# Modulation rows of the second block: products and sums on ACT, GpSimd and VectorE, with TensorE summing over the partitions

## The chip, the cores and the metric

One core of a Trainium2 chip runs the whole program. The metric is the time of one execution on the device in microseconds. Engines are named as in the profile: PE is TensorE (PEld its weight load), DVE is VectorE, ACT is ScalarE, POOL is GpSimd, SP is SyncE, whose queue issues most loads.

## The reference

The program computes two transformer blocks in float32. The first has two layers of a mixer and a SwiGLU FFN (512 tokens, width 1024, FFN width 2816). The second works on the result and on 256 context tokens, with a modulation of each of its two layers:

```python
silu_c, silu_cc = jax.nn.silu(c), jax.nn.silu(c_ctx)
for i in range(DEPTH):                      # 2 layers
    mod_l = silu_c @ ada_w[i] + ada_b[i]    # ada_w[i]: 1024 x 6144
    mod_c = silu_cc @ ada_w[i] + ada_b[i]
    sh1, sc1, gt1, sh2, sc2, gt2 = jnp.split(mod_l[:, None, :], 6, axis=-1)
    ...
```

So for each layer two vectors are multiplied with one matrix of 1024 rows and 6144 columns (24 MB). The inputs c and c_ctx do not depend on the first block, and the result is first needed in the second block.

## The kernel before, in words

The matrix is worked off inside the first block. `ada` (L1040) is a generator: each `next` sends one unit. For a layer there are 24 blocks of 256 columns. A unit loads one block of 1 MB (`adaw`, two buffers, one DMA on SP's queue), and sends eight matmuls on PE (L1053), one per group of 128 rows, with 32 columns of `cs` as the stationary operand (column 0 is silu(c), column 1 silu(c_ctx), the others zero). They go to four column groups of PE, so the result has four partial sums in four groups of 32 partitions. DVE copies it to `adap` (L1058). The next `next` sums the four groups and turns the row into a column by two matmuls with `sel` (L1061), and DVE adds the bias into `modT` (L1062). After the 24 blocks it scales and stores some rows, loads the router of the layer's mixture of experts (MoE), and folds the modulation into the router's bias.

The units are sent from `ada_step` (L1034), which `gemm_t` (L270) calls once per f-step. An f-step is one output tile of 128 columns by 512 tokens: 24 product matmuls, since each float32 product is made of three (L266 with xH and wH, L267 with xL and wH, L268 with xH and wL), for eight groups of 128 rows. Three of four f-steps send a unit, and one generator runs through both layers. The calls are in `ffn` (L525 and after), in the loop over blocks of the gate and the up weights. There, ACT makes the high part of a weight tile (L244) and DVE the low part (L245). For a gate tile DVE multiplies with the norm's factor (L530), ACT applies silu (L531), POOL multiplies with the factor once more (L532); for an up tile DVE multiplies into it (L535). The product tiles in PSUM are four buffers named `mmps`.

The order in which each engine gets its instructions is set by the scheduler of the framework, which moves units ahead of where the code sends them: in both kernels the first units of a layer stand before its FFN. For layer 0 that is the gated linear attention of the first mixer, GLA (lines L725 to L834), the output projection after it, and the residual (L359, L360, L370, L371, with a sum of squares by ACT L2800 and POOL L2807, the sum over partitions by PE L2820, the root by ACT L2811 and the reciprocal by DVE L2812, which gives `rstd`, the factor of the FFN's norm).

The lines that the steps of the prediction touch are those named here, and in GLA the ACT table loads at L729 and L730, DVE L731 to L744, POOL L746 and L749, and DVE L827.

## Time and profile before

| | before |
|---|---|
| median of 3 runs | 4202.54 us (4191.84 to 4209.45) |
| profiled execution | 4201.93 us |
| span of its trace | 4200.0 us |
| busy, PE | 3774.0 us (90%) |
| busy, DVE | 1838.8 us (44%) |
| busy, ACT | 1322.6 us (31%) |
| busy, POOL | 683.8 us (16%) |
| loads of the modulation matrix | 48 of 1024 KB, 5.0 us from issue to landing |

The span is the time between the first and the last instruction in the trace; 1.93 us lie around it. Busy shares are averages over stages with quite different limits, so each stage is read by itself. The line of an instruction is that of the kernel's file; a helper such as `mm3` has one line for all its callers, so the names of the tiles tell them apart. PE's matmuls are pipelined: what one costs is read from the distance between starts, not from its length.

### The profile page before, as it was taken

The numbers are of one execution on the slowest core, as the hardware profiler recorded it, in microseconds if no ns is written. First come the engines' busy times: TensorE is split into PE (matmuls) and PEld (weight loads), VectorE is DVE, ScalarE is ACT, GpSimd is POOL, SyncE is SP. The second block draws the span as 40 slices with busy tenths as digits, with TensorE's granted clock in tenths as the row PEclk, the third lists the DMA queues.
The fourth block names the chain that finished last, engine by engine and source line by source line (L and its number), as shares of the span: only waits on it lengthen the run. The fifth ranks groups of instructions, "written<-read, shape, count | busy, mean of one in ns | idle before, by whom it ended". The sixth has DMA issues, their size and how long they took to land. (4 is left out here: it accounts for less than half of the span.)

```text
span 4200.0 us, 56465 instructions
## 1 busy us (share of the span) xinstructions
PE 3774.0 (90%) x22550; PEld 2588.1 (62%) x22550; DVE 1838.8 (44%) x3646; ACT 1322.6 (31%) x2612; POOL 683.8 (16%) x889
## 2 busy tenths in 40 slices
PE   7979999999999979998789997996788899688986
PEld 6747778756777869887333334774667777433332
DVE  3445345565534545334422225445657655511112
ACT  3334224344323433233111113424456555200001
POOL 1002000200201010001100002002555342200001
PEclk9969999999999989999899998997768769799998
DMA  3213553212452322122799996342211212499997
GB/s 110 81 38 117 182 192 105 81 32 76 144 179 82 101 70 68 52 102 79 294 406 391 398 404 236 93 152 66 54 40 43 60 48 79 185 394 415 415 413 306
DMA packets 324825, 711.86 MB, mean 169 GB/s; under 512 B 79616, under 2 KB 251904, under 8 KB 299728
## 3 DMA queue, kind: packets, MB, share of 16 engines
q1 hardware_dynamic: 308704, 658.43, 43.1%
q0 software_dynamic: 15856, 49.79, 3.4%
q8 instruction: 179, 2.93, 0.3%
q14 instruction: 86, 0.70, 0.1%
HBM read 666.64 MB, written 47.55 MB: 170 GB/s over the span
## 5 line engine op out<-in xcount | busy, mean ns | idle before, releaser
L266 PE MATMUL mmps<-xH,wH 128*128 128x512 f32 (+1 forms) x1384 | 552.0, 401 | 11.2 <-ACT xH L359 9.4
L268 PE MATMUL mmps<-xH,wL 128*128 128x512 f32 (+1 forms) x1384 | 543.9, 394 | 2.4 <-DVE wL L245 2.4
L267 PE MATMUL mmps<-xL,wH 128*128 128x512 f32 (+1 forms) x1384 | 544.8, 394 | 0.0
L1488 PE MATMUL bgps<-wg,bxT 128*64 128x512 f32 (+2 forms) x1040 | 471.5, 597 | 0.9 <-issue 0.9
L1489 PE MATMUL bgps<-wu,bxT 128*64 128x512 f32 (+1 forms) x896 | 398.2, 597 | 21.1 <-DMA wu<-in_moe_w_up_dram 20.8
L244 ACT ACTIVATE wH<-wraw 128x512 fp32r<-128x512 f32 (+3 forms) x473 | 265.0, 620 | 481.4 <-PE mmps L267 270.6
L245 DVE TENSOR_TENSOR wL<-wraw,wH 128x512 fp32r<-128x512 f32 (+3 forms) x473 | 328.6, 739 | 193.6 <-ACT wH L244 193.0
L266 PEld LDWEIGHTS mmps<-xH,wH 128*128 128x128 f32 (+1 forms) x1384 | 259.9, 188 | 92.4 <-ACT wH L244 12.4
L268 PEld LDWEIGHTS mmps<-xH,wL 128*128 128x128 f32 (+1 forms) x1384 | 259.9, 188 | 66.1 <-DVE wL L245 3.9
L1505 PE MATMUL byps<-wd,bhT 128*64 128x512 f32 (+2 forms) x1040 | 297.0, 658 | 1.1 <-ACT bhT L1496 1.1
L267 PEld LDWEIGHTS mmps<-xL,wH 128*128 128x128 f32 (+1 forms) x1384 | 260.2, 188 | 59.9 <-issue 1.4
L1488 PEld LDWEIGHTS bgps<-wg,bxT 128*64 128x64 f32 (+2 forms) x1040 | 139.0, 137 | 206.7 <-issue 200.3
L1490 ACT ACTIVATE bh<-bgps 64x512 f32<-64x512 f32 (+2 forms) x65 | 38.3, 590 | 641.2 <-PE bgps L1489 543.0
L1489 PEld LDWEIGHTS bgps<-wu,bxT 128*64 128x64 f32 (+1 forms) x896 | 111.9, 128 | 132.7 <-issue 91.6
L1491 DVE TENSOR_TENSOR bh<-bgps,bh 64x512 f32<-64x512 f32 (+1 forms) x56 | 38.6, 690 | 335.7 <-ACT bh L1490 335.7
L1505 PEld LDWEIGHTS byps<-wd,bhT 128*64 128x64 f32 (+2 forms) x1040 | 87.9, 147 | 157.8 <-issue 152.1
L2420 POOL TENSOR_TENSOR isub<-xT,rwX 96x31 f32<-96x31 f32 (+15 forms) x248 | 140.6, 567 | 262.0 <-DMA xT<-rwd 243.2
L1454 POOL DMA_INDIRECT xg<-hnat,ix x65 | 62.8, 967 | 640.1 <-PE bxps L1476 602.9
L2424 POOL TENSOR_TENSOR rwX<-rwX,isub 96x31 f32<-96x31 f32 (+15 forms) x248 | 155.5, 627 | 19.4
L2807 POOL TENSOR_TENSOR sqs<-sqs,sq 128x512 f32<-128x512 f32 (+1 forms) x60 | 82.3, 1372 | 392.8 <-ACT sq L2800 386.4
L266 PE MATMUL mmps<-mH,pH 128*128 128x512 f32 (+2 forms) x336 | 124.1, 372 | 12.0 <-ACT pH L244 9.1
L532 POOL TENSOR_TENSOR ffng<-ffng,rstd 128x512 f32<-128x512 f32 x44 | 57.8, 1316 | 452.2 <-ACT ffng L531 439.9
(746 smaller groups left out, 7529.6 us busy)
## 6 DMA issues: line engine op xcount, KB each, us to landing
wg<-in_moe_w_gate_dram SPq DMA_DIRECT2D x64, 2048.0 KB, 23.1
wu<-in_moe_w_up_dram SPq DMA_DIRECT2D x61, 2048.0 KB, 20.1
wd<-in_moe_w_down_dram SPq DMA_DIRECT2D x61, 2048.0 KB, 19.2
adaw<-in_ada_w_dram SPq DMA_DIRECT2D x48, 1024.0 KB, 5.0
wraw<-in_ffn_w_gate_dram SPq DMA_DIRECT2D x22, 1024.0 KB, 5.4
wraw<-in_ffn_w_up_dram SPq DMA_DIRECT2D x22, 1024.0 KB, 5.5
wraw<-in_ffn_w_down_dram SPq DMA_DIRECT2D x20, 1024.0 KB, 5.0
wraw<-in_ga_w_in_dram SPq DMA_DIRECT2D x16, 1024.0 KB, 5.5
```

The source lines that it names most:

```text
L244: self.nc.scalar.activation(H, src, AF.Copy)
L245: self.nc.vector.tensor_tensor(L, src, H.bitcast(F32), OP.subtract)
L266: nc.tensor.matmul(out, lh, rh, start=first, stop=False)
L267: nc.tensor.matmul(out, lh, rl, start=False, stop=False)
L268: nc.tensor.matmul(out, ll, rh, start=False, stop=last)
L1454: self.gathered = self.nc.gpsimd.indirect_dma_start(out=x[:m, :], out_offset=None, in_=hnat, in_offset=bass.IndirectOffsetOnAxis(ap=it, ax ...
L1488: nc.tensor.matmul(og, xT[:, k, :m], wg[:, k, :], start=k == 0, stop=k == KD - 1, skip_group_check=True)
L1489: nc.tensor.matmul(ou, xT[:, k, :m], wu[:, k, :], start=k == 0, stop=k == KD - 1, skip_group_check=True)
L1505: nc.tensor.matmul(o[j], hT[:, k, :m], wd[:, k, j * 512 : (j + 1) * 512], start=k == 0, stop=k == 3, skip_group_check=True)
L2420: G.tensor_tensor(o, Lt[:96, :j, j : j + 1].to_broadcast((96, j, n)), X[:96, j : j + 1, j:].to_broadcast((96, j, n)), OP.mult,)
L2424: G.tensor_tensor(X[:96, :j, j:], X[:96, :j, j:], o, OP.add)
L2807: K.nc.gpsimd.tensor_tensor(self.acc, self.acc, t, OP.add)
```

## The change

The row sums move from PE to the other engines. A block has 512 columns now, 12 per layer, and is loaded in eight pieces of 128 rows (256 KB each, four buffers). For each piece ACT multiplies the tile by silu(c) of its rows (L1080), POOL adds that to `adac0` (L1081), and DVE multiplies by silu(c_ctx) and adds to `adac1` in one instruction (L1082); the first piece of a block is written by ACT (L1076) and DVE (L1077) directly. `adac0` and `adac1` have one buffer each. When a block is complete, PE sums both over the partitions by two matmuls with ones (L1052), ACT copies the result (L1054), and after a `yield` PE transposes it in four pieces (L1058) and DVE adds the bias (L1059). Each layer has its own generator, which must end in its own FFN, and an f-step sends one or two units of two pieces each. Lines of the changed kernel are one higher from the FFN on, and 23 higher behind `ada` (L2800, L2807, L2811, L2812 are now L2823, L2830, L2834, L2835).

```diff
@@ -539,12 +539,13 @@
                 (ev_gate, ev_up)[j // 2](j % 2, ps)
             ca = c.enter_context(ExitStack())
             self.adap = self.pool(f"ada{l}", ctx=ca)
+            self.ada_todo = self.ada(l)
             for b in range(256, FF, 256):
                 self.gemm_t(wg, b, b + 256, x, evac=lambda i, ps: ev_gate(b // P + i, ps), step=self.ada_step)
                 self.gemm_t(wu, b, b + 256, x, evac=lambda i, ps: ev_up(b // P + i, ps), step=self.ada_step)
+            assert next(self.ada_todo, self) is self
+            ca.close()
             if nxt is None:
-                assert next(self.ada_todo, self) is self
-                ca.close()
                 self.start_ctx()
             yp = self.pool(f"yffn{l}", ctx=c)
             yT = yp.tile([P, KD, T], F32, name="yT2")
@@ -1024,7 +1025,6 @@
         nc.scalar.activation(self.cs[:, :, 0], self.pvc("c_2", 0, 8), AF.Silu)
         nc.scalar.activation(self.cs[:, :, 1], self.pvc("c_ctx_2", 0, 8), AF.Silu)
         self.ada_n = 0
-        self.ada_todo = (u for l in range(2) for u in self.ada(l))
         late = self.cs.rearrange("p k i -> p (k i)")
         self.Lg, self.rtok = late[:, : TA // P * 36].rearrange("p (t e) -> p t e", e=36), late[:, TA // P * 36 : TA // P * 37]
         rcl = mp.tile([P, 2, 2, 36], F32, name="rcl")
@@ -1034,35 +1034,57 @@
     def ada_step(self):
 
         self.ada_n += 1
-        if self.ada_n % 4:
+        for _ in range(1 + self.ada_n % 2):
             next(self.ada_todo, None)
 
     def ada(self, l):
 
         nc = self.nc
         bias = self.pvc("ada_b_2", 48 * l, 48)
-        for b in range(24):
-            pool = self.adap
-            raw = pool.tile([P, 8, 256], F32, tag="adaw", name="adaw", bufs=2)
-            nc.sync.dma_start(
-                raw, self.io["ada_w_2"][l][:, b * 256 : (b + 1) * 256].rearrange("(k p) f -> p k f", p=P)
+        V, G, pool = nc.vector, nc.gpsimd, self.adap
+        w = self.io["ada_w_2"][l]
+        todo = []
+
+        def columns(b, acc):
+
+            ps = self.pp.tile([P, 512], F32, tag="sc", name="adps")
+            for i in range(2):
+                nc.tensor.matmul(ps[32 * i : 32 * i + 32, :], self.ones32, acc[i], start=True, stop=True, skip_group_check=True)
+            rows = pool.tile([P, 512], F32, tag="adar", name="adar")
+            nc.scalar.activation(rows[:64], ps[:64], AF.Copy)
+            yield
+            ps = self.pp.tile([P, 512], F32, tag="sc", name="adps")
+            for c in range(4):
+                nc.tensor.transpose(ps[:, c * 64 : (c + 1) * 64], rows[:64, c * P : (c + 1) * P], self.ident[:64, :64])
+            V.tensor_tensor(
+                self.modT[l][:, 4 * b : 4 * b + 4, :], ps[:, : 4 * 64].rearrange("p (c e) -> p c e", c=4)[:, :, 0::32],
+                bias[:, 4 * b : 4 * b + 4].unsqueeze(2).to_broadcast((P, 4, 2)), OP.add,
             )
-            ps = self.pp.tile([P, 512], F32, tag="sc", name="adps")
+
+        for b in range(12):
+            acc = None
             for k in range(KD):
-                j = 32 * (k % 4)
-                nc.tensor.matmul(
-                    ps[j : j + 32, :256], self.cs[:, k, :], raw[:, k, :],
-                    start=k < 4, stop=k >= 4, skip_group_check=True,
-                )
-            part = pool.tile([P, 256], F32, tag="adap", name="adap", bufs=2)
-            nc.vector.tensor_copy(part, ps[:, :256])
+                raw = pool.tile([P, 512], F32, tag="adaw", name="adaw", bufs=4)
+                nc.sync.dma_start(raw, w[k * P : (k + 1) * P, b * 512 : (b + 1) * 512])
+                if k % 2 == 0 and todo:
+                    next(todo[0], None)
+                    if k:
+                        todo.pop()
+                c0, c1 = (self.cs[:, k, i : i + 1] for i in range(2))
+                if k == 0:
+                    acc = [pool.tile([P, 512], F32, tag=f"adac{i}", name=f"adac{i}") for i in range(2)]
+                    nc.scalar.activation(acc[0], raw, AF.Copy, scale=c0)
+                    V.tensor_scalar(acc[1], raw, c1, None, OP.mult)
+                else:
+                    t = pool.tile([P, 512], F32, tag="adat", name="adat", bufs=2)
+                    nc.scalar.activation(t, raw, AF.Copy, scale=c0)
+                    G.tensor_tensor(acc[0], acc[0], t, OP.add)
+                    V.scalar_tensor_tensor(acc[1], raw, c1, acc[1], OP.mult, OP.add)
+                if k % 2:
+                    yield
+            todo.append(columns(b, acc))
+        for _ in todo[0]:
             yield
-            for j in range(2):
-                nc.tensor.matmul(ps[:, 256 + 2 * j : 258 + 2 * j], part[:, j * P : (j + 1) * P], self.sel, start=True, stop=True)
-            nc.vector.tensor_tensor(
-                self.modT[l][:, 2 * b : 2 * b + 2, :], ps[:, 256:260].rearrange("p (m i) -> p m i", i=2),
-                bias[:, 2 * b : 2 * b + 2].unsqueeze(2).to_broadcast((P, 2, 2)), OP.add,
-            )
...
-        rows = self.adap.tile([P, 256], F32, tag="adap", name="adap", bufs=2)
+        rows = self.adap.tile([P, 512], F32, tag="adar", name="adar")
         nc.vector.tensor_copy(rows[:48, :P], ps[:48, :P])
         nc.sync.dma_start(self.modR[l], rows[:48, :P])
 
-        wr, ws = (self.adap.tile([P, 8, 256], F32, tag="adaw", name="adaw", bufs=2) for _ in range(2))
-        self.load_router(l, wr[:, :, :36])
+        wr, ws = (self.adap.tile([P, 512], F32, tag="adaw", name="adaw", bufs=4) for _ in range(2))
+        wr = wr[:, : KD * 36].rearrange("p (k e) -> p k e", k=KD)
+        self.load_router(l, wr)
         nc.sync.dma_start(self.rcl[l], self.io["moe_b"][l : l + 1, :].unsqueeze(1).to_broadcast((P, 2, 36)))
         yield
         ps = self.pp.tile([P, 512], F32, tag="sc", name="adps")
-        v = ws[:, :, :72].rearrange("p k (i e) -> p k i e", e=36)
         for i in range(2):
-            nc.vector.tensor_tensor(v[:, :, i], wr[:, :, :36], F[:, 1, i, :].unsqueeze(2).to_broadcast((P, KD, 36)), OP.mult)
-        sums = wr[:, 0, 64:136]
-        nc.vector.tensor_reduce(sums, ws[:, :, :72].rearrange("p k e -> p e k"), axis=AX.X, op=OP.add)
+            v = ws[:, : KD * 36].rearrange("p (k e) -> p k e", k=KD)
+            nc.vector.tensor_tensor(v, wr, F[:, 1, i, :].unsqueeze(2).to_broadcast((P, KD, 36)), OP.mult)
+            nc.vector.tensor_reduce(rows[:, P + 36 * i : P + 36 * i + 36], v.rearrange("p k e -> p e k"), axis=AX.X, op=OP.add)
+        sums = rows[:, P : P + 72]
         nc.tensor.matmul(ps[:, :72], self.ones, sums, start=True, stop=True)
         nc.vector.tensor_tensor(self.rcl[l], self.rcl[l], ps[:, :72].rearrange("p (i e) -> p i e", e=36), OP.add)
```

PE inside the FFN's gate and up loop, before: one unit between two f-steps.

```order
L267 MATMUL mmps<-xL_2192,wH 128x512
L268 MATMUL mmps<-xH_2191,wL 128x512
L1061 MATMUL adps<-small,adap 128x2 x2
L1053 MATMUL adps<-adaw,cs 32x256 x8
L266 MATMUL mmps<-xH_2191,wH 128x512
L267 MATMUL mmps<-xL_2192,wH 128x512
L268 MATMUL mmps<-xH_2191,wL 128x512
```

PE inside the same loop, in the changed kernel: the sums of one block and its transposes (`adac` are the sums, `adar` the copied row).

```order
L268 MATMUL mmps<-xH_2191,wL 128x512
L1052 MATMUL adps<-adac_3444,ones 32x512
L1052 MATMUL adps<-adac_3445,ones 32x512
L266 MATMUL mmps<-xH_2191,wH 128x512
L267 MATMUL mmps<-xL_2192,wH 128x512
L268 MATMUL mmps<-xH_2191,wL 128x512
L266 MATMUL mmps<-xH_2191,wH 128x512
L267 MATMUL mmps<-xL_2192,wH 128x512
L268 MATMUL mmps<-xH_2191,wL 128x512
L1058 MATMUL adps<-ident,adar 128x64 x4
L266 MATMUL mmps<-xH_2191,wH 128x512
L267 MATMUL mmps<-xL_2192,wH 128x512
```

The old unit stood after each of three f-steps out of four. The pairs of sums now stand 48, 72, 72 and again 48 product matmuls apart; transposes follow six (as here) or 24 product matmuls after the sums.

DVE in the same loop of the changed kernel, between two pairs of sums that are 48 product matmuls apart; before, the only instructions of the modulation among them were one L1058 and one L1062 per unit.

```order
L245 TENSOR_TENSOR wL<-wraw,wH 128x512
L1077 TENSOR_SCALAR adac_3609<-adaw,cs 128x512
L245 TENSOR_TENSOR wL<-wraw,wH 128x512
L1082 SCALAR_TENSOR_TENSOR adac_3609<-adaw,cs,adac_3609 128x512
L1059 TENSOR_TENSOR modT_81<-adps,pv 128x8
L1082 SCALAR_TENSOR_TENSOR adac_3609<-adaw,cs,adac_3609 128x512
L245 TENSOR_TENSOR wL<-wraw,wH 128x512
L1082 SCALAR_TENSOR_TENSOR adac_3609<-adaw,cs,adac_3609 128x512
L245 TENSOR_TENSOR wL<-wraw,wH 128x512
L1082 SCALAR_TENSOR_TENSOR adac_3609<-adaw,cs,adac_3609 128x512 x2
L530 TENSOR_TENSOR fg<-mmps,rstd 128x512
L1082 SCALAR_TENSOR_TENSOR adac_3609<-adaw,cs,adac_3609 128x512 x2
L530 TENSOR_TENSOR fg<-mmps,rstd 128x512
L245 TENSOR_TENSOR wL<-wraw,wH 128x512
```

All products of a block (L1077 and L1082) stand between the weight tiles' low parts (L245), with the bias addition of the block before (L1059) among them.

DVE at the end of the residual before the first FFN, before:

```order
L360 SCALAR_TENSOR_TENSOR xL_2192<-xT,pv,xH_2191 128x512
L1062 TENSOR_TENSOR modT_81<-adps,pv 128x4
L1058 COPY adap<-adps 128x256
L360 SCALAR_TENSOR_TENSOR xL_2192<-xT,pv,xH_2191 128x512
L2812 RECIPROCAL rstd<-rstd 128x512
L530 TENSOR_TENSOR fg<-mmps,rstd 128x512 x2
L245 TENSOR_TENSOR wL<-wraw,wH 128x512 x2
```

and in the changed kernel:

```order
L1059 TENSOR_TENSOR modT_81<-adps,pv 128x8
L360 SCALAR_TENSOR_TENSOR xL_2192<-xT,pv,xH_2191 128x512
L1082 SCALAR_TENSOR_TENSOR adac_3000<-adaw,cs,adac_3000 128x512
L360 SCALAR_TENSOR_TENSOR xL_2192<-xT,pv,xH_2191 128x512
L1082 SCALAR_TENSOR_TENSOR adac_3000<-adaw,cs,adac_3000 128x512 x5
L2835 RECIPROCAL rstd<-rstd 128x512
L530 TENSOR_TENSOR fg<-mmps,rstd 128x512 x2
L245 TENSOR_TENSOR wL<-wraw,wH 128x512 x2
```

Before the reciprocal that gives `rstd` there are six products in place of one copy and one addition. On ACT four scaled copies (L1080) stand ahead of the root (L2834) at the same place, and on POOL five adds (L1081) stand ahead of L746 and two between L746 and L749 in GLA.

## Rows read from the trace of the kernel before

**Rows 1.** Windows: us, busy of PE PEld DVE ACT POOL (instructions), PEclk, DMA share, GB/s.
```profile
400.00:655.00 255.00, 253.74 (x1433) 200.67 (x1432) 104.19 (x184) 60.15 (x110) 28.52 (x22) 1.00 0.54 178
1100.00:1345.00 245.00, 243.87 (x1256) 191.67 (x1256) 95.39 (x162) 55.88 (x102) 29.05 (x22) 1.00 0.45 143
```

**Rows 2.** PE's waits in the first FFN stage: us in total, times, longest.
```profile
PE mmps L268 <- DVE wL L245: 1.3, 1, 1.3
```

**Rows 3.** Timeline, PE, first FFN: start, length, engine line op, out<-in, count [idle before].
```profile
434.77 0.50 PE L266 MATMUL mmps<-xH,wH 128*128 128x512 f32 x1
...
445.81 0.50 PE L1061 MATMUL adps<-small,adap 128*128 128x2 f32 x4
...
447.24 0.50 PE L266 MATMUL mmps<-xH,wH 128*128 128x512 f32 x1
...
452.83 0.17 PE L1061 MATMUL adps<-small,adap 128*128 128x2 f32 x1
```

**Rows 4.** Timeline, PE, second layer's mixer: a pair of column sums.
```profile
835.49 0.39 PE L268 MATMUL mmps<-xH,wL 128*128 128x512 f32 x1
835.81 1.05 PE L334 MATMUL sqp<-sq,ones 128*32 128x512 f32 x4
836.79 0.50 PE L266 MATMUL mmps<-xH,wH 128*128 128x512 f32 x1
```

**Rows 5.** Timeline, PE, MoE stage: transposes of the same shape.
```profile
2092.85 1.04 PE L1476 MATMUL bxps<-ident,xg 64*128 64x64 f32 x8
2093.82 1.08 PE L1505 MATMUL byps<-wd,bhT 128*64 128x512 f32 x4
```

**Rows 6.** Timeline, PE, ahead of the first FFN: two sums after each other.
```profile
391.86 1.02 PE L2820 MATMUL msp<-sqs,ones 128*128 128x512 f32 x2
...
393.81 0.40 PE L267 MATMUL mmps<-xL,wH 128*128 128x512 f32 x1
```

**Rows 7.** Timeline, ACT, residual before the first FFN: one scaled copy.
```profile
388.56 0.72 ACT L359 ACTIVATE xH<-xT,pv 128x512 fp32r<-128x512 f32 x1 [3.54 <-POOL xT L371]
```

**Rows 8.** Timelines, POOL and DVE: each beside the other, then each alone.
```profile
20.84 9.69 POOL L2807 TENSOR_TENSOR sqs<-sqs,sq 128x512 f32<-128x512 f32 x6 [18.27 <-ACT sq L2800]
...
21.40 9.67 DVE L360 SCALAR_TENSOR_TENSOR xL<-xT,pv,xH 128x512 fp32r<-128x512 f32 x6 [0.38 <-ACT xH L359]
...
435.11 1.29 POOL L532 TENSOR_TENSOR ffng<-ffng,rstd 128x512 f32<-128x512 f32 x1 [4.28 <-ACT ffng L531]
...
389.31 0.75 DVE L360 SCALAR_TENSOR_TENSOR xL<-xT,pv,xH 128x512 fp32r<-128x512 f32 x1 [1.53 <-ACT xH L359]
```

**Rows 9.** Groups of DVE by shape, 400 to 650: busy us, mean ns | idle before.
```profile
L245 DVE TENSOR_TENSOR wL<-wraw,wH 128x512 fp32r<-128x512 f32 x83 | 63.1, 802 | 0.2 <-ACT wH L244 0.2
...
L530 DVE TENSOR_TENSOR fg<-mmps,rstd 128x512 f32<-128x512 f32 x20 | 13.8, 690 | 78.5 <-PE mmps L268 78.5
```

**Rows 10.** GLA stage: window (columns as rows 1), and timelines of PE, DVE, ACT, POOL.
```profile
244.00:311.00 67.00, 48.56 (x179) 29.94 (x178) 28.12 (x68) 23.48 (x54) 4.69 (x2) 0.54 0.09 29
...
262.85 1.23 PE L787 MATMUL atps<-glaQ,glaK 64*128 64x128 f32 x8 [16.05 <-DVE glaK L744]
...
253.94 0.69 DVE L732 TENSOR_TENSOR glala<-glala,ge 128x512 f32<-128x512 f32 x1 [3.28 <-ACT ge L730]
...
249.95 1.28 ACT L729 ACT_TABLE_LOAD   x1
...
258.23 2.35 POOL L746 TENSOR_TENSOR glaQ<-qb,glaQ 128x1024 f32<-128x1024 f32 x1 [20.11 <-ACT glaQ L745]
```

**Rows 11.** Timelines, ACT and DVE, from the residual into the first FFN.
```profile
393.78 0.69 ACT L2811 ACTIVATE rstd<-msp,small 128x512 f32<-128x512 f32 x1 [3.98 <-PE msp L2820]
...
394.50 3.35 DVE L2812 RECIPROCAL rstd<-rstd 128x512 f32<-128x512 f32 x1 [4.43 <-ACT rstd L2811]
```

**Rows 12.** DMA issues, 0 to 1400: count, KB each, median us to landing.
```profile
wraw<-in_ffn_w_gate_dram SPq DMA_DIRECT2D x22, 1024.0 KB, 5.4
...
tab<-in_cst_dram POOLq DMA_DIRECT2D x8, 256.0 KB, 3.0
```

## Prediction

> **What bounds the kernel now.** I read the windows view first, then PE's waits, then the groups by shape, and at last the timelines of single stretches. The matrix of the second block is worked off inside the gate and up loops of the first block's two FFNs. In those two stages PE is busy for 253.74 of 255.00 us and for 243.87 of 245.00 us, at a granted clock of 1.00, while DVE is at 104.19, ACT at 60.15 and POOL at 28.52 [rows 1]. PE's waits add up to 1.3 us over the whole first stage [rows 2]. So a microsecond of PE work taken out there is a microsecond of the kernel, and work for DVE, ACT and POOL is free until one of them makes PE wait.
>
> **What goes from PE.** In a run of product matmuls, 24 of them lie between 447.24 and 452.83 (5.59 us) and 48 between 434.77 and 445.81 (11.04 us) [rows 3]. The difference gives 0.227 us for a matmul and leaves 0.14 us for restarting after something else. An old unit (two small matmuls with sel, eight with the columns of cs) stands from 445.81 to 447.24, 1.43 us; with the restart 1.57 us. There are 48 of them, two for each new block of 512 columns: 3.14 us a block.
>
> The new block has two sums with a ones operand of 32 columns, and four transposes of 64x128. No row shows them for this matrix, so I take the nearest shapes. A pair of sums with the same shape, in two column groups, holds up the stream from 835.49 + 0.23 to 836.79, 1.07 us, with restart 1.21 [rows 4]. Eight half passes 64\*128 64x64, which are four such transposes, take 2092.85 to 2093.82, 0.97 us, with restart 1.11 [rows 5]. Together 2.32 us a block, 0.82 less than before; if the two sums ran one after the other, the pair would cost what two sums of 128\*128 cost, from 391.86 to 393.81 less one matmul of 0.23 [rows 6], 1.72, with restart 1.86, and the gain would shrink to 0.17. Of the 24 blocks some five are sent before the FFN, where PE is not full. 19 x 0.82 = 15.6, 24 x 0.82 = 19.7; I take **-17 us**.
>
> **What comes to the other engines.** 192 scaled copies on ACT, 168 adds on POOL, 192 scaled products on DVE (168 of them scalar_tensor_tensor with two inputs in SBUF). A scaled copy takes 0.72 [rows 7], so 138 us more on ACT over 500 us with 116 busy: no bound. A POOL add takes 1.29 alone and a scalar_tensor_tensor 0.75 alone [rows 8]. They do not run freely beside each other: in one stretch POOL needs 9.69 us for six adds and DVE 9.67 us for six scalar_tensor_tensors at the same time [rows 8], where six alone would be 7.7 and 4.5. So a pair costs 9.69 / 6 = 1.615 us, with either engine held up by the other. DVE's subtraction L245 is of the same kind (two SBUF inputs, 802 ns in the mean [rows 9]), while L530 with a PSUM input keeps 690 ns [rows 9].
>
> The rule in the Trainium skill, page "SBUF — State Buffer", section "Who interferes with whom", speaks against this change more strongly: a VectorE instruction with two SBUF inputs and a GpSimd instruction that reads SBUF exclude each other, and the loser blocks for the whole instruction. By it the sum would come to 4278, the end that is worked out under the first rival. The trace agrees that they hold each other up, and differs on the size: 1.615 us for a pair is less than the two durations alone, 2.04.
>
> **The wait that is added.** adac0 and adac1 have one buffer. The first copy of block b+1 must wait until PE has read block b, and PE's next pair of sums must wait for the seventh add of POOL and the last product of DVE: PE and the three helpers meet once per block. In the new order the pairs stand 48, 72, 72 product matmuls apart. With 72 PE needs 72 x 0.227 + 1.11 + 0.14 = 17.6 us, with 48 it needs 48 x 0.227 + 1.11 + 0.14 = 12.2 us. The helpers need: the copy L1054 and the two copies L1076 and L1080 on ACT, at 0.72 each 2.2; seven adds, contested throughout, 7 x 1.615 = 11.3; the last product 0.75; together 14.2 us. So each 48-matmul interval stalls PE by some 2 us, and there are three per layer: **+12 us**. If the adds were never contested, 2.2 + 7 x 1.29 + 0.75 = 12.0 us, no stall (lower bound 0). An interval of 72 holds one or two adds L532 more: 14.2 + 2 x 1.615 = 17.5 against 17.6, just hidden.
>
> **What moves before the FFN.** Layer 0's first units are sent in the GLA stage (244 to 311), where the granted clock is 0.54 and PE waits 16.05 us for a chain over ACT, DVE and POOL [rows 10]. Eight DVE operations now stand within it (8 x 0.75 = 6.0 at most, nothing if they fall into waits such as that of 3.28 ahead of L732), and POOL has five adds ahead of L746, after 20.11 us of idling, and two more ahead of L749 (2 x 1.615 = 3.2); two table loads of 1.28 go (L729 and a second one). Between -2.6 and 6.0 + 3.2 = +9.2; I take **+4**, near the middle. At 313 us the addition L1059 now stands ahead of L827 on DVE and waits for sums, copy and transposes: 1.21 + 0.72 + 1.11 = 3.0 [rows 4, 5, 7], less what hides of it: 0 to 3, taken **+2**. Around the two output projections one to three products of DVE stand ahead of the splits that PE waits for: 1 to 3 x 0.75, taken **+2.5** for both.
>
> Between residual and FFN, rstd goes PE, ACT L2811, DVE L2812 (3.35 us), L530 [rows 11]. Ahead of it there now stand up to four scaled copies on ACT, each behind a load of 256 KB (3.0 us from issue to landing for a load of that size [rows 12]) into one of four buffers, and six products on DVE, five of them behind its last split, with adds of POOL beside them. PE is not waiting there now, but its product tiles are full until L530 empties them. 5 x 0.75 = 3.8 is the least and 5 x 1.615 = 8.1 the most if nothing were done earlier; I take 4 for layer 0 and 3 for layer 1, **+7**; nothing at the low end if the products end before PE's sum.
>
> The 20 small loads ahead of the first gate weight on SP's queue, and 9 or 10 between weight loads later, I cost at nothing: they are the same bytes, weights come 5.4 us after issue [rows 12], and an f-step pair takes 11 us. If that cover is gone, each weight load is late by the wait of one adaw buffer.
>
> **Sum.** -17 + 12 + 4 + 2 + 2.5 + 7 = +10.5 against the profiled execution of 4201.93: 4212.4. The median of the three runs is 0.6 higher; I say **4213 us**. What a measurement of this kernel can tell from no change is some 0.5%, 21 us, so the likeliest outcome is no difference. Its own range is 4193 (half of the stalls, and 2 us of the rest) to 4223.
>
> **The rivals.**
> *The helpers are the bound everywhere (slower).* The term is the pair price. An interval of 72 has only 0.1 us of slack at 1.615; from (17.6 - 2.95) / 9 = 1.63 us a pair on, or with one add more in it, every block stalls PE. If one waited for the whole of the other, 1.29 + 0.75 = 2.04 a pair, the 48-intervals need 2.2 + 14.3 + 0.75 = 17.2 (stall 5.0, six of them 30) and the 13 others 2.2 + 18.4 + 0.75 = 21.3 (stall 3.7, 48 together): 4201.9 - 17 + 78 + 15.5 = 4278. Halfway between that and the forecast, 4245. For it: DVE and POOL alternate strictly in rows 8. Against: DVE is only at 104 of 255 and its order has waits for PE in which POOL's adds run alone. Chance 0.22 for over 4223.
> *The sums run one after the other, or loads come late (slower).* The change then does not take off PE what it says: -0.17 x 24 = -4 in place of -17, 4225; a weight load late by 5 us once per layer gives 10 more. Chance 0.18 for these together above 4223.
> *Only the PE term counts (faster).* The adds fall into DVE's pauses, the chain of GLA loses its two table loads, rstd is not late: -17 - 2.6, 4182. For it: PE is the only full engine [rows 1]. Against: the meeting once per block. With half of the waits: 4192. Chance 0.12 for a gain of over 21 us, which needs the largest PE term, 19.7, beside it (4180).
>
> **How the numbers follow.** Forecast within 21 us of before: 0.48; slower by over 0.5%: 0.40; faster: 0.12. The range takes in the faster rival, 4182, and at the top the halfway price of the first with the sums one after the other: 4245 + 13 = 4258.
>
> **What would show it.** In the profile after: PE's busy time in the two FFN stages lower by some 8 us each; PE waits on L1052 for POOL L1081 or DVE L1082, about 2 us each and about six times; a mean of L1081 well over 1.29 us and of L1082 over 0.75; rstd later by 3 to 4 us after the residual; the GLA stage longer by some 4 us. Waits at L1052 at every block would mean the first rival; no wait at L1052 the last. The prediction is wrong in mechanism if PE waits in the FFN for weights (L244, L245 behind the scaled copies or the products) instead.

## The result, and the profile after

The changed kernel takes **4238.89 us** (median of 16 runs) against 4202.22 us before (16 runs): ratio **1.0099, interval 1.0077 to 1.0121**, some 32 to 51 us slower. The forecast was 4213 us, with no difference from before (21 us either way) as the likeliest case and a range up to 4258: the range held, the likeliest case did not come. The profiled execution was 4225.5 us with a span of 4223.7 us.

The page of the profile after, its part 1 (busy us, share, instructions), has less PE work and more of everything else:

```profile
PE 3737.6 (88%) x21782; PEld 2544.7 (60%) x21782; DVE 2097.5 (50%) x3768; ACT 1463.3 (35%) x2826; POOL 973.5 (23%) x1057
```

The windows over the two FFN stages (columns as in [rows 1]):

```profile
400.00:655.00 255.00, 238.12 (x998) 178.78 (x997) 205.75 (x219) 114.51 (x188) 139.77 (x90) 0.96 0.49 156
1100.00:1345.00 245.00, 230.72 (x957) 167.17 (x956) 215.15 (x216) 119.73 (x196) 153.35 (x97) 0.98 0.49 155
```

DVE has doubled, POOL is five times as busy, PE has pauses, and the granted clock is no longer 1.00. PE's waits in the two stages (us in total, times, longest; first 420 to 680, then 1125 to 1393), where before there was 1.3 us in the first [rows 2]:

```profile
PE adps L1052 <- POOL adac L1081: 8.6, 3, 4.8
PE mmps L266 <- DVE fg L530: 4.7, 1, 4.7
PE adps L1052 <- DVE adac L1082: 1.5, 2, 1.2
...
PE adps L1052 <- POOL adac L1081: 8.5, 3, 4.2
...
PE adps L1052 <- DVE adac L1082: 1.8, 3, 1.2
```

So the sums wait for POOL's last add and DVE's last product, six times, 20.4 us. All six are at the intervals of 48 product matmuls; none at one of 72. In three of them no load was late. Ahead of the three longest ACT had waited for a load of the modulation matrix: 4.08 us ahead of the one at 593.09 (on ACT, POOL and PE below), 4.06 ahead of that at 1244.44, 2.50 ahead of that at 1301.04.

```profile
584.44 0.73 ACT L1080 ACTIVATE adat<-adaw,cs 128x512 f32<-128x512 f32 x1 [4.08 <-DMA adaw<-in_ada_w_dram]
...
585.31 1.84 POOL L1081 TENSOR_TENSOR adac<-adac,adat 128x512 f32<-128x512 f32 x1 [2.58 <-ACT adat L1080]
...
593.09 1.91 PE L1052 MATMUL adps<-adac,ones 128*32 128x512 f32 x3 [4.76 <-POOL adac L1081]
```

That load was issued late, at 581.65: SP's queue had stood 5.2 us for a weight buffer that DVE's L245 had to free, and then 3.5 us for a modulation buffer that DVE's L1077 had to free.

Another of the six on PE's timeline (start, length):

```profile
480.12 1.04 PE L1052 MATMUL adps<-adac,ones 128*32 128x512 f32 x2 [1.73 <-POOL adac L1081]
482.34 1.91 PE L1052 MATMUL adps<-adac,ones 128*32 128x512 f32 x2 [1.18 <-DVE adac L1082]
484.18 0.80 PE L266 MATMUL mmps<-xH,wH 128*128 128x512 f32 x1
...
485.20 0.63 PE L268 MATMUL mmps<-xH,wL 128*128 128x512 f32 x1
485.63 0.63 PE L266 MATMUL mmps<-xH,wH 128*128 128x512 f32 x1
...
488.87 0.39 PE L268 MATMUL mmps<-xH,wL 128*128 128x512 f32 x1
489.10 0.40 PE L266 MATMUL mmps<-xH,wH 128*128 128x512 f32 x1
```

The wait is not all. Behind it the product matmuls start 0.43 us apart in place of 0.23, until 488.6. The windows before, in and after that stretch show the granted clock (the third number from the end is PEclk; 0.50 is 1.2 GHz, 1.00 is 2.4 GHz):

```profile
465.70:480.00 14.30, 12.69 (x56) 9.23 (x56) 14.19 (x14) 7.17 (x12) 11.15 (x7) 1.00 0.45 144
484.00:488.60 4.60, 4.60 (x11) 3.47 (x11) 4.24 (x5) 3.93 (x7) 3.24 (x3) 0.50 0.41 125
488.60:503.40 14.80, 14.80 (x67) 11.72 (x65) 13.31 (x14) 6.63 (x11) 8.78 (x6) 1.00 0.57 183
```

An interval of 72 matmuls without such a wait ahead of it takes 18.15 us in FFN 0 and 18.55 in FFN 1, from the start of one pair of sums to the start of the next. The six behind a wait take 23.31, 20.92, 20.69 and 20.77, 22.24, 21.34 us: 10.5 and 8.7 us too much, 19.2 together. Three things are in these 19.2 us:

- 3.3 us are DVE's part of the 20.4 us of waits, which falls between the two sums of a pair.
- Some 11 us are the clock. The granted clock in the six is 0.85, 0.92, 0.88 and 1.00, 0.88, 0.92 on average, 0.50 for 3 to 7 us in five of them. Half of the time that PE was busy at 0.50 gives the 11 us, an estimate.
- The rest, some 5 us, is that the second sum runs after the first and not beside it.

The fourth interval shows the last by itself. Its clock stayed at 1.00, and it is 2.2 us too long: 1.18 are a wait, 1.0 is the second sum (the pair holds PE from 1187.31 to 1190.51, an undisturbed one from 503.43 to 504.41).

```profile
1187.31 1.04 PE L1052 MATMUL adps<-adac,ones 128*32 128x512 f32 x2 [1.51 <-POOL adac L1081]
1189.53 1.05 PE L1052 MATMUL adps<-adac,ones 128*32 128x512 f32 x2 [1.18 <-DVE adac L1082]
1190.51 0.50 PE L266 MATMUL mmps<-xH,wH 128*128 128x512 f32 x1
```
```profile
1187.31:1208.08 20.77, 19.59 (x81) 14.00 (x81) 20.63 (x20) 9.89 (x17) 14.08 (x9) 1.00 0.53 170
```

The groups of POOL and DVE in FFN 0 (420 to 680; busy us, mean ns), to be held against [rows 8, 9]:

```profile
L1081 POOL TENSOR_TENSOR adac<-adac,adat 128x512 f32<-128x512 f32 x63 | 101.1, 1605 | 28.6 <-ACT adac L1076 16.6 <-ACT adat L1080 8.1
L1082 DVE SCALAR_TENSOR_TENSOR adac<-adaw,cs,adac 128x512 f32<-128x512 f32 x63 | 86.6, 1374 | 3.1 <-DMA adaw<-in_ada_w_dram 2.0
L245 DVE TENSOR_TENSOR wL<-wraw,wH 128x512 fp32r<-128x512 f32 x84 | 79.7, 984 | 4.8 <-ACT wH L244 4.8
```

Ahead of the FFN, `rstd` is late by about as much as forecast. On ACT and DVE (to be held against [rows 11]):

```profile
408.96 0.72 ACT L1080 ACTIVATE adat<-adaw,cs 128x512 f32<-128x512 f32 x1 [2.25 <-DMA adaw<-in_ada_w_dram]
...
414.67 0.72 ACT L1080 ACTIVATE adat<-adaw,cs 128x512 f32<-128x512 f32 x1 [0.68 <-DMA adaw<-in_ada_w_dram]
415.30 0.67 ACT L2834 ACTIVATE rstd<-msp,small 128x512 f32<-128x512 f32 x1
...
406.90 5.80 DVE L1082 SCALAR_TENSOR_TENSOR adac<-adaw,cs,adac 128x512 f32<-128x512 f32 x5
416.00 3.35 DVE L2835 RECIPROCAL rstd<-rstd 128x512 f32<-128x512 f32 x1 [3.30 <-ACT rstd L2834]
```

The root waits behind four copies, each of which waits for its load (5.8 us in all). DVE had its products done at 412.70 and waited 3.30 us for the root, and PE then waits 4.7 us for L530.

Where the time went, by stages, each from starts in the timelines (us). "Second before" is the kernel before in a second profiled execution, run as an experiment below; "no POOL", "pace" and "best" are experiments too.

| stage | before | second before | after | pace | no POOL | best |
|---|---|---|---|---|---|---|
| start to GLA (L725 in the kernel before) | 244.8 | 251.8 | 249.4 | 250.6 | 250.5 | 251.3 |
| GLA's chain, to PE L787 | 18.0 | 18.0 | 24.1 | 24.1 | 20.2 | 18.0 |
| from there to the first L530 | 135.1 | 134.8 | 145.9 | 146.4 | 140.6 | 135.6 |
| FFN 0, first L530 to last L535 | 259.7 | 259.6 | 260.2 | 246.4 | 246.2 | 245.4 |
| to the first L530 of FFN 1 | 439.1 | 439.1 | 444.7 | 444.4 | 437.7 | 438.1 |
| FFN 1, first L530 to last L535 | 252.2 | 252.2 | 267.9 | 253.3 | 250.0 | 249.7 |

From GLA to the end of FFN 1 the change costs 6.1 + 10.8 + 0.6 + 5.5 + 15.7 = 38.7 us, close to the 36.7 between the medians.

### The profile page after: what moved, and what is told of

The parts are those of the page before. It is cut to its first block, busy times and chain, and to the rows that moved or that the text cites. A ratio compares the mean times of both kernels' runs of the same rounds, so it can differ in the third digit from the quotient of the medians.

```text
span 4223.7 us, 56138 instructions
## 1 busy us (share of the span) xinstructions
PE 3737.6 (88%) x21782; PEld 2544.7 (60%) x21782; DVE 2097.5 (50%) x3768; ACT 1463.3 (35%) x2826; POOL 973.5 (23%) x1057
## 5 line engine op out<-in xcount | busy, mean ns | idle before, releaser
L266 PE MATMUL mmps<-xH,wH 128*128 128x512 f32 (+1 forms) x1384 | 558.0, 405 | 23.4 <-ACT xH L359 14.3
L1511 PE MATMUL bgps<-wg,bxT 128*64 128x512 f32 (+2 forms) x1040 | 473.0, 600 | 0.9 <-issue 0.9
L245 DVE TENSOR_TENSOR wL<-wraw,wH 128x512 fp32r<-128x512 f32 (+3 forms) x473 | 362.1, 807 | 186.7 <-ACT wH L244 186.1
L266 PEld LDWEIGHTS mmps<-xH,wH 128*128 128x128 f32 (+1 forms) x1384 | 263.3, 191 | 112.9 <-issue 23.4
L1081 POOL TENSOR_TENSOR adac<-adac,adat 128x512 f32<-128x512 f32 x168 | 271.2, 1614 | 140.1 <-ACT adac L1076 92.0
L1511 PEld LDWEIGHTS bgps<-wg,bxT 128*64 128x64 f32 (+2 forms) x1040 | 139.8, 137 | 216.2 <-issue 209.8
L1082 DVE SCALAR_TENSOR_TENSOR adac<-adaw,cs,adac 128x512 f32<-128x512 f32 x168 | 226.6, 1349 | 10.3 <-DMA adaw<-in_ada_w_dram 7.3
L2443 POOL TENSOR_TENSOR isub<-xT,rwX 96x31 f32<-96x31 f32 (+15 forms) x248 | 152.3, 614 | 228.7 <-DMA xT<-rwd 209.9
L1080 ACT ACTIVATE adat<-adaw,cs 128x512 f32<-128x512 f32 x168 | 119.4, 721 | 158.9 <-POOL adac L1081 100.8
L2447 POOL TENSOR_TENSOR rwX<-rwX,isub 96x31 f32<-96x31 f32 (+15 forms) x248 | 155.1, 625 | 19.5
## 6 DMA issues: line engine op xcount, KB each, us to landing
wd<-in_moe_w_down_dram SPq DMA_DIRECT2D x61, 2048.0 KB, 19.1
```

Source lines behind the costliest of these rows:

```text
L245: self.nc.vector.tensor_tensor(L, src, H.bitcast(F32), OP.subtract)
L266: nc.tensor.matmul(out, lh, rh, start=first, stop=False)
L1081: G.tensor_tensor(acc[0], acc[0], t, OP.add)
L1082: V.scalar_tensor_tensor(acc[1], raw, c1, acc[1], OP.mult, OP.add)
L1511: nc.tensor.matmul(og, xT[:, k, :m], wg[:, k, :], start=k == 0, stop=k == KD - 1, skip_group_check=True)
L2443: G.tensor_tensor(o, Lt[:96, :j, j : j + 1].to_broadcast((96, j, n)), X[:96, j : j + 1, j:].to_broadcast((96, j, n)), OP.mult,)
```

## The experiments

The theory: PE and its helpers meet once per block, the six short intervals make PE wait, and a wait is followed by a stretch at half clock. Rivals: POOL and DVE hold each other up so much that the helpers are too slow at any pace; the chain of copies and loads is what is late; what counts is the work sent ahead of the FFN.

**A more even pace.**
```diff
-        for _ in range(1 + self.ada_n % 2):
+        for _ in range(1 + (self.ada_n % 4 == 1)):
```


> Only the pace changes: of four f-steps one sends two units and three send one, so two pairs of sums are never closer than 72 product matmuls (in the changed kernel they stand 48, 72, 72 apart). Theory (one meeting per block): the six waits at L1052 in the 48-matmul intervals (18 us together) and the stretches at a lower granted clock behind them (some 19 us) both go; PE waits at L1052 under 4 us in both FFN stages together, granted clock 0.99 or more in them, from the first L535 to the last 245 us in each FFN (256.7 and 264.4 now), time 25 to 35 us under the changed kernel, about 4208. Rival (POOL and DVE hold each other up so much that the helpers are too slow at any pace): the waits come back at the 72-matmul intervals, time unchanged, about 4239.

Measured: 4211.15 us, ratio to the kernel before 1.0028 (1.0000 to 1.0056). The FFN stages fall from 260.2 and 267.9 to 246.4 and 253.3, 28.4 us together. PE's waits in FFN 0 and FFN 1:
```profile
PE adps L1052 <- POOL adac L1081: 3.8, 1, 3.8
...
PE adps L1052 <- POOL adac L1081: 4.6, 2, 2.6
```
That is 8.7 us with 0.3 for DVE, more than the 4 expected, and three intervals of 72 still have one, each behind a load that ACT had waited 4.3 to 5.1 us for. The theory holds in the main. The means of the adds and products are as before (1616 and 1373 ns), so with the same adds and products the time changes with where PE meets them. The edit also spreads the blocks, from 64 to 77 product matmuls a block in the mean. This run does not part the two; that the changed kernel has no wait at its intervals of 72 speaks for the short ones.

**Two buffers for each sum** (paid for with the fourth load buffer, and the copied row takes a buffer of `adat`).
```diff
-                raw = pool.tile([P, 512], F32, tag="adaw", name="adaw", bufs=4)
+                raw = pool.tile([P, 512], F32, tag="adaw", name="adaw", bufs=3)
...
-            rows = pool.tile([P, 512], F32, tag="adar", name="adar")
+            rows = pool.tile([P, 512], F32, tag="adat", name="adar", bufs=2)
...
-                    acc = [pool.tile([P, 512], F32, tag=f"adac{i}", name=f"adac{i}") for i in range(2)]
+                    acc = [pool.tile([P, 512], F32, tag=f"adac{i}", name=f"adac{i}", bufs=2) for i in range(2)]
```


> The two sums adac0 and adac1 get two buffers each, paid for in SBUF by three load buffers in place of four and the copied row in adat's buffers; the pace stays at 48, 72, 72 (50, 70, 72). Theory (one meeting per block): the next block no longer waits for PE, so the helpers work across the block's border: PE waits at L1052 under 6 us in both FFN stages together (20 now), clock 0.98 or more, time 20 to 35 us under the changed kernel, about 4210. Rival (helpers too slow in the mean): the waits stay between 12 and 20 us, time about 4235. If the third load buffer is missed, waits of L1080 and L1082 for loads go up from some 25 us.

Measured: 4271.95 us, ratio 1.0170 (1.0128 to 1.0212): a miss, much slower. The FFN stages take 277.1 and 284.9 us, and the waits at L1052 grew to 57 us:
```profile
PE adps L1052 <- POOL adac L1081: 28.7, 6, 10.0
...
PE adps L1052 <- POOL adac L1081: 28.5, 3, 9.9
```
The price in SBUF was worse than the gain. To part the two prices, **three load buffers alone:**
```diff
-                raw = pool.tile([P, 512], F32, tag="adaw", name="adaw", bufs=4)
+                raw = pool.tile([P, 512], F32, tag="adaw", name="adaw", bufs=3)
```


> The changed kernel with three load buffers in place of four, nothing else; to settle why two buffers for the sums, paid for with the fourth load buffer and with adar in adat's buffers, gave waits of 57 us at L1052. Theory (three load buffers are too few): DVE's waits for loads at L1082 rise from 2 to over 25 us in an FFN stage, PE's waits at L1052 to 35 us or more in both together, FFN stages 270 us or more. Rival (the copied row among ACT's product tiles was the fault): waits as in the changed kernel, 20 us, FFN stages 260 and 268 us.

Measured in one execution (4209.62 us; its stages alone are read): waits at L1052 of 13.4 and 11.2 us (24.6 in all, 20.4 with four), FFN stages of 263.8 and 271.0. DVE's waits for loads are up from 2 to 18 us:
```profile
L1082 DVE SCALAR_TENSOR_TENSOR adac<-adaw,cs,adac 128x512 f32<-128x512 f32 x63 | 81.1, 1287 | 19.0 <-DMA adaw<-in_ada_w_dram 18.2
```
That is between what the theory and its rival had. So one load buffer fewer costs some 7 us in the FFN stages; the other 27 of the run before came with the copied row among ACT's products, or with the second buffers themselves. This was not parted further.

**No product before the FFN's factor is there.**
```diff
+            self.ada_cs = self.adap.tile([P, KD, 2], F32, name="adcs")
+            nc.vector.scalar_tensor_tensor(
+                self.ada_cs, r[:, : 2 * KD].rearrange("p (k i) -> p k i", i=2), 0.0, self.cs[:, :, :2], OP.mult, OP.add
+            )
             self.ada_todo = self.ada(l)
...
-                c0, c1 = (self.cs[:, k, i : i + 1] for i in range(2))
+                c0, c1 = (self.ada_cs[:, k, i : i + 1] for i in range(2))
```


> The two vectors are copied by one small DVE instruction that also reads rstd, so no product can start before the FFN's norm factor is there; pace and buffers as in the changed kernel. Theory (work sent ahead of the FFN costs some 17 us in layer 0 without the chance part, and 5.5 us in layer 1): the first L530 of layer 0 falls from 419.5 to 398 to 403 us, the stretch from the last L535 of FFN 0 to the first L530 of FFN 1 shrinks from 444.7 to 439 to 441, and both FFN stages grow by 2.5 blocks of some 2 us of PE work and one or two more waits with their slow clock, 8 to 14 us each; time 0 to 10 us under the changed kernel, about 4234. Rival (the work ahead of the FFN is hidden, and the delay there is chance): the stages before the FFN stay as late, time 15 to 25 us above the changed kernel, about 4259.

Measured: 4240.47 us, ratio 1.0098 (1.0066 to 1.0131), the same as the changed kernel. The first L530 of layer 0 comes at 404.9 (the second execution of before has 404.7), the stretch between the FFNs takes 436.4; but the FFN stages grow to 278.3 and 279.5, in FFN 0 by more than expected. So all the delay ahead of the FFN is the work sent there, and with the helpers as they are that work costs as much inside the FFN.

**DVE makes both sums, ACT and POOL none.**
```diff
-                    nc.scalar.activation(acc[0], raw, AF.Copy, scale=c0)
+                    V.tensor_scalar(acc[0], raw, c0, None, OP.mult)
...
-                    t = pool.tile([P, 512], F32, tag="adat", name="adat", bufs=2)
-                    nc.scalar.activation(t, raw, AF.Copy, scale=c0)
-                    G.tensor_tensor(acc[0], acc[0], t, OP.add)
+                    V.scalar_tensor_tensor(acc[0], raw, c0, acc[0], OP.mult, OP.add)
```


> DVE makes both sums with two products in place of ACT's copy, POOL's add and one product; ACT and POOL get nothing of the modulation. Theory (POOL and DVE hold each other up): the mean of L1082 falls from 1.4 to 0.70 us, L532 on POOL back to 1.30, L245 to 0.80; a block costs DVE 14 x 0.7 + 1.0 = 10.8 us, with its weight work of some 4 to 5 us per two f-steps 15 us against 12.2 of PE in a short interval, so the waits at L1052 stay at some 2 us, 10 to 18 together, time 0 to 15 us under the changed kernel, about 4232. Rival (what counts is only how much DVE has to do in order): DVE's wL (L245) comes late, PE waits at L268 or L266 for it over 10 us, time above the changed kernel, over 4250.

Measured: 4181.02 us, ratio 0.9990 (0.9957 to 1.0024): no slower than the kernel before, and better than I expected. Waits at L1052 of 3.5 and 1.9 us, granted clock 1.00 in both FFN windows, no wait for wL; L532 on POOL stays at 1660 ns, against what I expected.

**One word: DVE adds in place of POOL**, ACT's chain as it is.
```diff
-                    G.tensor_tensor(acc[0], acc[0], t, OP.add)
+                    V.tensor_tensor(acc[0], acc[0], t, OP.add)
```


> One word of the changed kernel differs: the addition L1081 is done by DVE, ACT still makes the scaled copies with two buffers. Theory (POOL's adds are slow, and they and DVE's products hold each other up): as in the form with two products on DVE, means of L1081 and L1082 at 0.7 to 0.8 us, waits at L1052 under 6 us in both FFN stages together, clock 1.00, time 30 to 40 us under the changed kernel, ratio to the kernel before 0.997 to 1.003. Rival (the chain of ACT copies, its two buffers and the loads is what is late): the waits at L1052 stay at 15 to 20 us with ACT adat L1080 ahead of them, ratio 1.006 to 1.010.

Measured: 4193.15 us, ratio 1.0008 (0.9982 to 1.0034). The groups in FFN 0 and PE's waits in both:
```profile
L1082 DVE SCALAR_TENSOR_TENSOR adac<-adaw,cs,adac 128x512 f32<-128x512 f32 x63 | 56.0, 889 | 0.2
...
L1081 DVE TENSOR_TENSOR adac<-adac,adat 128x512 f32<-128x512 f32 x63 | 43.1, 684 | 1.2 <-ACT adat L1080 0.9
```
```profile
PE adps L1052 <- DVE adac L1081: 2.4, 3, 0.8
...
PE adps L1052 <- DVE adac L1081: 1.8, 3, 0.6
```
An add takes 0.68 us on DVE and took 1.6 on POOL, and DVE's own products became faster too, with all of both on one engine. The copies and loads are as they were, and ACT even waits longer for loads (26.6 us in FFN 0, 16.6 in the changed kernel), yet a sum waits at most 0.8 us. So late loads by themselves do not make PE wait; POOL's adds are the cause, and a late load lengthens a chain that they have left no room in.

**What POOL and DVE do to each other**, by itself: in the gated run DVE's sum stands in PSUM, so its product has one SBUF input.
```diff
-                    V.tensor_scalar(acc[1], raw, c1, None, OP.mult)
+                    part = self.pp.tile([P, 512], F32, tag="tp", name="adpp")
+                    V.tensor_scalar(part, raw, c1, None, OP.mult)
...
-                    V.scalar_tensor_tensor(acc[1], raw, c1, acc[1], OP.mult, OP.add)
+                    V.scalar_tensor_tensor(part if k < KD - 1 else acc[1], raw, c1, part, OP.mult, OP.add)
```


> The run with the gate, and in it DVE adds its products up in a PSUM tile (only the last of eight writes adac1 in SBUF), so that DVE's product has one input in SBUF in place of two; POOL still does its adds, pace and buffers are those of the changed kernel. To be compared with the gated run (FFN stages 278.3 and 279.5 us, ratio 1.0098). Theory (two SBUF inputs of DVE's product and POOL's add hold each other up): L1082's mean falls from 1.4 to about 0.7 us, L1081's from 1.6 to 1.3 to 1.45 (L245 still contends), a block's adds take 9.5 to 10 us in place of 11.3, the waits at L1052 fall by at least half, the FFN stages to 252 to 265 us each; ratio 1.000 to 1.006. Rival (POOL's adds are what is slow, by themselves): L1081 stays at 1.55 to 1.65, the FFN stages over 272 us, ratio 1.008 to 1.011.

Measured: ratio 1.0106 (1.0073 to 1.0139), FFN stages 272.7 and 276.3 against 278.3 and 279.5. The groups of the gated run, then of this one:
```profile
L1085 POOL TENSOR_TENSOR adac<-adac,adat 128x512 f32<-128x512 f32 x78 | 124.7, 1598 | 30.4 <-ACT adac L1080 13.0 <-ACT adat L1084 12.8
L1086 DVE SCALAR_TENSOR_TENSOR adac<-adaw,adcs,adac 128x512 f32<-128x512 f32 x79 | 105.7, 1338 | 5.5 <-DMA adaw<-in_ada_w_dram 4.2
```
```profile
L1086 POOL TENSOR_TENSOR adac<-adac,adat 128x512 f32<-128x512 f32 x77 | 109.0, 1415 | 38.7 <-ACT adac L1080 18.9 <-ACT adat L1085 15.1
...
L1087 DVE SCALAR_TENSOR_TENSOR adpp<-adaw,adcs,adpp 128x512 f32<-128x512 f32 x65 | 48.9, 752 | 31.3 <-DMA adaw<-in_ada_w_dram 30.3
```
That POOL and DVE hold each other up is shown: with one SBUF input fewer DVE's product falls from 1338 to 752 ns and POOL's add from 1598 to 1415. The expected effect did not follow: the sums still wait 23.4 and 19.9 us. The trace says why. At the two short intervals without a late load on ACT, at 470.2 and 1182.4 us, the sums wait 0.5 and 0.3 us (2.4 to 2.9 in the changed kernel where no load was late). The four long waits, 10.8, 8.1, 10.2 and 6.4 us, each stand behind a load that ACT had waited 4.3 to 4.6 us for, the first of them after SP's queue had stood 11.5 us for a weight buffer:
```profile
527.89 0.72 ACT L1085 ACTIVATE adat<-adaw,adcs 128x512 f32<-128x512 f32 x1 [4.46 <-DMA adaw<-in_ada_w_dram]
...
530.08 1.92 PE L1056 MATMUL adps<-adac,ones 128*32 128x512 f32 x4 [10.77 <-POOL adac L1086]
```
Both the theory and its rival missed: the hold-up is real, and loads that come late hid what it is worth. Why the loads are later here than in the gated run was not tested.

**The clock behind a wait.** Useless matmuls fill the waits at the short intervals.
```diff
             ps = self.pp.tile([P, 512], F32, tag="sc", name="adps")
+            if b in (3, 6, 9):
+                for _ in range(12):
+                    nc.tensor.matmul(ps, self.H[:, 0, :P], self.H[:, 0, :], start=True, stop=True)
             for i in range(2):
```


> The changed kernel with work added that nobody needs: ahead of the sums of blocks 3, 6 and 9 of each layer, those of the short intervals, PE does 12 product-shaped matmuls (128x512, 12 x 0.227 = 2.7 us, 16.3 us in all six places) into the tile that the sums then overwrite. Theory (the wait at the sums leaves PE idle, and behind it PE runs at a lower granted clock, which costs as much again): the added matmuls fill the waits (1.9, 2.3, 4.9, 1.7, 4.4, 3.0 us), of which 4 us in all remain, the next intervals of 72 matmuls fall from 20.7 to 23.3 us back to 18.2 and 18.6 where the wait was under 3 us, and the FFN stages become shorter in spite of the added work: 252 to 257 and 260 to 265 us (260.2 and 267.9 now), time 5 to 15 us under the changed kernel, ratio 1.006 to 1.009. Rival (the long intervals behind the waits have another cause, weights or PE's own loads): the stages stay or grow by up to 8 us each, ratio 1.010 to 1.014.

Measured: the FFN stages take 258.4 and 262.6 us with 16.3 us of added work, 7.1 us less than the changed kernel without it. The windows 412 to 680 and 1110 to 1390, of this run and then of the changed kernel:
```profile
412.00:680.00 268.00, 255.66 (x1107) 196.68 (x1106) 206.02 (x229) 120.17 (x200) 137.52 (x87) 0.99 0.48 155
1110.00:1390.00 280.00, 269.00 (x1150) 201.03 (x1148) 221.37 (x239) 129.93 (x216) 151.28 (x97) 1.00 0.48 151
```
```profile
412.00:680.00 268.00, 252.10 (x1064) 191.31 (x1064) 209.42 (x228) 120.40 (x201) 134.97 (x86) 0.96 0.48 153
1110.00:1390.00 280.00, 265.32 (x1100) 194.95 (x1099) 222.40 (x235) 124.44 (x204) 149.10 (x95) 0.98 0.47 146
```
The granted clock is back, and the intervals of 72 behind take 19.5, 18.7, 20.4 and 19.7, 19.1, 19.1 in place of 20.7 to 23.3 us: 6.3 us over the undisturbed ones in place of 19.2. Of the 12.9 us that are gone 1.8 are waits of DVE between the sums, and 11.1 the clock, as estimated above; what is left, at a clock of 1.00, are such waits (1.5) and sums that run one after the other (4.8). Idle time at the sums is what lowered the clock. The whole time missed its forecast: 4245.64 us, ratio 1.0142 (1.0102 to 1.0183). Its interval meets that of the changed kernel, and the stages outside the FFNs differ between executions by more than the 7 us at stake, so the run tells of the stages only.

**Putting it together.** DVE alone; the two tiles of ACT's copies are given up for a second buffer of each sum; the even pace:
```diff
-                    acc = [pool.tile([P, 512], F32, tag=f"adac{i}", name=f"adac{i}") for i in range(2)]
+                    acc = [pool.tile([P, 512], F32, tag=f"adac{i}", name=f"adac{i}", bufs=2) for i in range(2)]
...
-        for _ in range(1 + self.ada_n % 2):
+        for _ in range(1 + (self.ada_n % 4 == 1)):
```


> DVE makes both sums alone, the sums have two buffers each (the two tiles of ACT's copies are given up for them, loads keep four buffers), and of four f-steps one sends two units. Theory (one meeting per block): the remaining waits at L1052 (5.4 us with one buffer) go, under 1.5 us in both FFN stages together, clock 1.00; one more block is sent ahead of each FFN, so the first L530 of layer 0 comes 2 to 5 us later than with one buffer (411.4), the FFN stages are 3 to 6 us shorter each (246.2 and 250.0); time like or up to 8 us under the one-buffer form, ratio to the kernel before 0.995 to 1.000. Rival (the load buffers and not the sums' buffers hold the chain): waits unchanged, time the same as the one-buffer form.

Measured: 4183.74 us, ratio 0.9971 (0.9942 to 1.0000), no wait at the sums in the FFN stages, which take 238.2 and 242.7 us; a block more is sent ahead of each FFN, and the first L530 comes at 414.5. **With the gate as well:**

> As the run with two buffers and DVE alone, and in addition no product starts before the FFN's rstd. Theory: the first L530 of layer 0 falls to 398 to 405 us, between the FFNs 436 to 438 us, the FFN stages take 249 to 256 us each (all 12 blocks in them, 1.8 us of PE a block, no waits at L1052 over 1 us); from the start to the end of FFN 1 some 8 us less than the kernel before, ratio to it 0.994 to 0.999: faster than both kernels. Rival (DVE in the FFN is too full when all blocks are there): L245 late, PE waits for wL over 5 us, ratio over 1.000.

Measured: 4172.76 us, ratio **0.9967 (0.9938 to 0.9996)**, and once more:

> The form with DVE alone, two buffers per sum, the even pace and the gate once more, to narrow its interval (0.9967, 0.9938 to 0.9996): 0.994 to 0.999, faster than the kernel before by 5 to 25 us. If it is not faster, the ratio comes out at 0.999 or above.

Measured: 4177.81 us, ratio **0.9963 (0.9935 to 0.9992)**. It is the best version: faster than both kernels, by some 15 us against the kernel before (0.0035 of 4200) and, by the difference of the ratios (0.0134), some 56 against the changed one. The column "best" above is its first run.

**The kernel before once more:**

> The kernel before once more, unchanged, for a second profile: is the 4.6 us that the changed kernel and its variants have lost by the start of the gated linear attention (at 178 to 186 us, in which no instruction of the modulation runs, at a granted clock of 0.50 in place of 1.00) a property of the change or of the single execution? If of the execution: GLA starts between 244.8 and 251 here too. If of the change: at 244.8 again, within 0.5 us.

Measured: GLA starts at 251.8 us, with the same code as at 244.8. The windows 178 to 188 of the first execution of before, of the changed kernel and of this one:
```profile
178.00:188.00 10.00, 9.89 (x51) 5.74 (x50) 7.48 (x25) 4.59 (x15) 0.54 (x1) 1.00 0.54 159
```
```profile
178.00:188.00 10.00, 10.00 (x25) 4.82 (x24) 5.88 (x21) 3.28 (x11) 0.59 (x2) 0.50 0.34 101
```
```profile
178.00:188.00 10.00, 9.65 (x24) 4.48 (x23) 7.33 (x22) 5.42 (x15) 1.07 (x2) 0.62 0.20 52
```
The 4.6 us that the changed kernel has lost there belong to the execution, not to the change. So does the stretch between the two MoE stages of the second block, from the last L1488 of the first (L1511 in the changed kernel) to the first of the second: 1108.3 us in the first execution of before, 1085.4 in the second, 1085.3 in the changed kernel. That is why the profiled spans differ by only 23.7 us and the medians by 36.7.

## Why the prediction was right or wrong

**PE's saving, -17: right in size, in part by luck.** With waits of 0.3 us at the sums and all 12 blocks in its FFN, the best version's FFN stages are 14.3 and 2.5 us shorter than before, 16.8. A block costs PE less than I had it, 18.15 - 72 x 0.227 = 1.8 us in FFN 0 and, with matmuls 0.233 us apart there, 1.8 in FFN 1, against 2.32. The price that was off is that of the four transposes: I took the eight of [rows 5] for four, 0.97 us, and they hold PE for 0.39 (1175.34 to 1175.73):

```profile
1175.34 0.46 PE L1058 MATMUL adps<-ident,adar 64*128 64x64 f32 x4
1175.73 0.51 PE L266 MATMUL mmps<-xH,wH 128*128 128x512 f32 x1
```

So a block saves 1.3 us, not 0.82. That the sum still came out right is because the gain falls unevenly, which I did not see: before, 24 of the 48 units stood in FFN 0, some 15 in FFN 1 and 9 outside both, so layer 1's FFN takes in more work than it had.

**The stalls, +12: right place, mis-sized.** They are at L1052, in the six short intervals, on POOL's seventh add and DVE's last product, as the step "each 48-matmul interval stalls PE by some 2 us" says; but 20.4 us in all, 3.4 each. The pair price of 1.615 us was right for POOL (1605 ns in the mean; the 1.29 that [rows 8] call alone had DVE's L245 beside it from 435.25 on, two of which took 2.30 us, so it is POOL's time when it is not held up); but DVE's L245 and L530 stand between the products, and the second sum waited for DVE by itself (1.18 us on the timeline above). And the loads, which the prediction cost "at nothing", did come late: not the weight loads, as it feared, but the modulation's own loads behind them on SP's queue, ahead of the three longest waits (4.76, 4.50 and 3.08 us; the other three are 2.4 to 2.9).

**The term that was missing: what follows a wait.** "PE needs 17.6 us for 72 matmuls" takes 0.227 us a matmul for granted. Behind five of the six waits PE ran at half clock for some microseconds (behind three of them the product matmuls too, 0.43 us apart): some 11 us. The sums of a pair that DVE is late for run one after the other, some 5 us more; the prediction had a price for that (0.65 us a pair), but in a rival and not in the sum. The row to read for the clock was in my hands: in GLA's window, with PE busy for 48.56 of 67 us, the granted clock is 0.54 [rows 10]; I had used it only for GLA.

**Ahead of the FFN, +15.5 in four terms: right in kind, short by a third.** GLA's chain +6.1 (+4 forecast); between the FFNs +5.5 (+4: 3 for rstd, 1 for the projection). From GLA's chain to the first L530 of layer 0 it is +10.8 (+7.5: 2 at 313 us, 1.5 for the projection, 4 for rstd). Of these PE's wait for L530 was 4.7 us, close to the 4, but by another path: I had priced DVE's products, and what came last was ACT's copies behind their loads, which DVE waited 3.30 us for. The addition at 313 us, forecast at +2, cost at most half a microsecond, as PE's last L833 (L834 in the changed kernel) ended 53.2 us after the first L787 before and 53.4 after; so the projection and the residual cost more than I had them. The gated run shows that all of it is the work sent there.

**The rivals.** The first (helpers the bound everywhere) did not come: no interval of 72 of the changed kernel had a wait. POOL's adds came at 1.605 us in the mean, DVE's products at 1.374, not at 2.04, and with one of its inputs in PSUM DVE's product was back at 0.75. The Trainium skill, page "SBUF — State Buffer", section "Who interferes with whom", says that an instruction of VectorE with at most one SBUF input does not contend with GpSimd; the PSUM run agrees, with 0.75. The same section calls the shared ports an exclusive lock, by which the prediction had the time at 4278; the measured means are shorter than its 2.04 a pair. The second rival came in part: the two sums did run one after the other where DVE was late, and loads were late for ACT's copies, though no weight load for PE. The third (only the PE term counts) is what came when POOL was left out.

**In sum**: forecast +10.5, found +38.7 from GLA to the end of FFN 1. Of the missing 28 the clock has some 11, the waits 8.4, the work ahead of the FFNs 6.9 and the sums one after the other some 5. The 3 that these are too many are PE's saving: the changed kernel's two FFN stages are 16.3 us longer with 36 us of waits, clock and late sums in them, so PE's own work there fell by 20 and not 17. Slower by over 0.5% had 0.40, no difference 0.48. That the range held is luck in part: its upper end, 4258, was added up from a higher pair price at every block, which did not come, and sums one after the other at every block, which came only at the waits; the term that filled it, the clock, was not in it.
